# Three feed-forward blocks begun for the first token tile, and a last chunk that skips its round trip

## The chip, the cores and the metric

The kernel runs on one core of one Trainium2 chip. The metric is the device time of one execution in microseconds, taken from several runs, of which the median is quoted. The names of the engines are those of the profile: PE is the matrix engine (TensorE), PEld its weight loads, DVE is VectorE, ACT is ScalarE, POOL is GpSimd, SP is SyncE, which here only issues transfers. Each engine works through its own list of instructions in order and waits on semaphores for the others.

## The reference, cut to what matters

One encoder block with `D_MODEL = 2048`, 256 tokens, all in float32. Two branches (a gated linear attention and a convolution branch called Hyena) are merged, projected, added to the input and normalised; a feed-forward part with a squared ReLU follows.

```python
y_gla = _gla_branch(q, k, v, r, af, ab, ...)
y_hy = _hyena_branch(hy_u, ...)
merged = g[:, :, 0, :] * (y_gla @ w_gla_o[l]) + g[:, :, 1, :] * (y_hy @ w_hy_o[l])
mix = merged @ w_out[l]
h = _layernorm(DEEPNORM_ALPHA * h + mix, ln1_g[l], ln1_b[l])
ff = jnp.square(jax.nn.relu(h @ w_ff1[l])) @ w_ff2[l]
h = _layernorm(DEEPNORM_ALPHA * h + ff, ln2_g[l], ln2_b[l])
```

`w_ff1` is 2048 x 8192 and `w_ff2` 8192 x 2048. The layer norm needs the mean and variance of each token's whole row of 2048 values, so nothing of `h @ w_ff1` can begin for a token before that token's row of `mix` is complete.

## The kernel before, in words

**High and low parts.** Every float32 operand is split in two (`split_hi_lo`, line 82): the high part is a copy in a type that the matrix engine reads fast (an ACT cast, line 83), the low part is the difference to the original (a DVE subtraction, line 84). A product is then three: high by high, high weight by low activation, and low weight by high activation.

**Weights.** They come as 302 blocks of 128 x 2048 (1 MB) through `fetch` (line 91): SP loads a block into one of three `raw` buffers, ACT and DVE split its two halves into three `whi` and three `wlo` buffers of half a block each. `next_block` fetches one block more and hands out the oldest. `resident` (line 838) does the same for blocks that get a place of their own in a slot that is otherwise used for something else.

**Channel products.** With the weights as stationary operand and the activations of both token tiles as moving one, `channel_pair` computes 2 x 128 output channels for all 256 tokens. A block gives 128 channels: 16 high products with 512 moving columns (high and low activation of 256 tokens, line 144) and 16 low products with 256 columns (line 148). `channel_sum` (line 153) adds both column groups. `channel_pair_by_tokens` is a form for the first pair alone: its first one and a half blocks are computed for the first 128 tokens, then again for the second 128, so that high products have 256 columns and low products 128.

**The passage from projection to feed-forward.** The output projection (`wo` in the profile) is done in four groups of 512 output columns. For the last group three blocks are made resident (`x0` and `wr`), so that the first token tile can be finished (`column_products`, lines 885 to 887) before the second. For each token tile follow: `add_mix` (line 901, with the statistics in line 903), `norm_scale` (lines 857 to 861, with the short instructions of lines 214 to 219), five chunks of `norm_chunk` (an ACT scaling in line 868, a DVE product in line 869 and, for the first tile alone, a DVE addition in line 871), and for each chunk `turn`: transposes on PE (line 928; for the second tile also a product that adds the bias, line 932) into a PSUM buffer `ht`, and a split into `hT` (lines 83 and 84). There are four such PSUM buffers (`sdp`) and five chunks. Then `ff1(0)` begins.

**Slots.** The tag `xT` of the pool `base` holds one tile at a time: first the input, then `mT`, the moving operand of the projection, later feed-forward activations. A new tile in the slot waits for the last reader of the one before.

**Order.** The program is written engine-free; a scheduler (`schedule_with_timeline_sim`) sets the order on each engine at build time, except inside `tc.high_priority()`, which moves instructions ahead, and a few fixed places. On the chip the order on each engine is then fixed.

**The Hyena output.** Each of its eight chunks ends in `hy_inv` (line 727): a product on DVE gives `yo`, which goes to DRAM (`yd`) by a POOL transfer. After the gate products `g2` all eight are read back (`yr`) and split into `yhT`, the moving operand of the products `ho`.

## Time and profile before

| | us |
|---|---|
| median of 3 runs | 1862.57 (1861.92 to 1862.78) |
| the profiled execution | 1862.62 |
| its span, first to last instruction | 1860.8 |
| PE busy | 1852.2 |
| DVE busy | 1286.1 |
| ACT busy | 934.5 |

The profiled execution's time is 1.8 us longer than its span: what lies around the first and last instruction. Times in the views are microseconds from the start of the span. The end of a matrix product is modelled by the profile and lies after the start of the next one, so the time that a row of products takes on PE is read from start to start and not from their durations. On DVE and ACT the next instruction starts a little before the end of the one ahead of it, so there too the step is read from start to start.

### The profile page before, as it was taken

Reading aid. Unit: us, or ns where it says so; the run is one execution under the profiler, and the core shown is the slowest. Engines: PE = TensorE matmul, PEld = TensorE weight load, DVE = VectorE, ACT = ScalarE, POOL = GpSimd, SP = SyncE. Lnnn points to the kernel's source line nnn. Section 1 sums busy time; section 2 is a strip of 40 time slices with the busy share of each in tenths; the row PEclk is TensorE's granted clock in tenths of the full one; section 3 lists DMA queues with packets and bytes.
Section 4 is the critical chain, followed back from the end, with each engine's and each line's share of the span. In section 5 each row is a group of like instructions: output and inputs, shape, how many; then the busy total and the mean of one; then the engine's idle time right before and its main releaser. Section 6 shows DMA issues by size and latency. Waiting matters only on the chain.

```text
span 1860.8 us, 23989 instructions
## 1 busy us (share of the span) xinstructions
PE 1852.2 (100%) x9471; PEld 1576.7 (85%) x9471; DVE 1286.1 (69%) x1628; ACT 934.5 (50%) x1268; POOL 30.8 (2%) x61
## 2 busy tenths in 40 slices
PE   9999999999999999999999999999999999999999
PEld 7888888888888888888888889888888888888887
DVE  6787878765788988888645567666555554665557
ACT  5555558765555555555444445444434443444332
POOL 1000000000000000000000000000000000000000
PEclk9999999999999999999999999999999999999999
DMA  7677664445555555566555764555545554545553
GB/s 286 235 251 263 243 233 168 157 159 195 191 199 193 195 217 190 203 218 222 197 188 193 277 219 156 194 209 192 193 186 199 183 197 186 201 184 188 196 192 125
DMA packets 59536, 375.51 MB, mean 202 GB/s; under 512 B 6720, under 2 KB 9184, under 8 KB 20000
## 3 DMA queue, kind: packets, MB, share of 16 engines
q1 hardware_dynamic: 46080, 324.03, 47.2%
q0 software_dynamic: 6288, 30.16, 4.4%
q10 hardware_dynamic: 7056, 19.80, 2.8%
q8 instruction: 74, 1.21, 0.3%
q14 instruction: 38, 0.31, 0.0%
HBM read 357.19 MB, written 16.78 MB: 201 GB/s over the span
## 4 chain that ended last, share of the span: by engine, by line
PE 98%; DVE 1%; DMA 0%; ACT 0%; issue 0%; SPq 0%; DVEq 0%
PE f L144 12%; PE f L148 7%; PE w L198 6%; PE w L197 6%; PE w L196 6%; PE uz L144 3%; PE uv L144 3%; PE ux L144 3%; PE g L196 3%; PE g L198 3%; PE g L197 3%; PE uv L148 2%; PE ux L148 2%; PE uz L148 2%; PE k L144 2%; PE r L196 2%
## 5 line engine op out<-in xcount | busy, mean ns | idle before, releaser
L84 DVE TENSOR_TENSOR wlo<-raw,whi 128x1024 fp32r<-128x1024 f32 x590 | 720.0, 1223 | 351.8 <-ACT whi L83 350.4
L83 ACT CAST whi<-raw 128x1024 fp32r<-128x1024 f32 x590 | 619.6, 1051 | 490.6 <-PE w L198 188.2
L144 PE MATMUL f<-hT,whi 128*128 128x512 f32 (+1 forms) x1048 | 246.4, 386 | 0.0
L144 PEld LDWEIGHTS f<-hT,whi 128*128 128x128 f32 x1048 | 190.1, 188 | 35.6
L197 PE MATMUL w<-wlo,f 128*128 128x512 f32 x480 | 186.7, 389 | 0.0
L198 PE MATMUL w<-whi,f 128*128 128x512 f32 x480 | 186.7, 389 | 0.0
L196 PE MATMUL w<-whi,f 128*128 128x512 f32 x480 | 167.4, 389 | 0.0
L148 PEld LDWEIGHTS f<-hT,wlo 128*128 128x128 f32 x1048 | 134.1, 191 | 4.8
L148 PE MATMUL f<-hT,wlo 128*128 128x256 f32 (+1 forms) x1048 | 135.8, 282 | 0.0
L156 ACT ACTIVATE f_l<-f 128x256 f32<-128x256 f32 x64 | 24.5, 384 | 163.8 <-PE f L144 163.8
L197 PEld LDWEIGHTS w<-wlo,f 128*128 128x128 f32 x480 | 90.1, 188 | 18.7
L196 PEld LDWEIGHTS w<-whi,f 128*128 128x128 f32 x480 | 90.1, 188 | 18.7
L198 PEld LDWEIGHTS w<-whi,f 128*128 128x128 f32 x480 | 90.1, 188 | 18.7
L157 DVE SCALAR_TENSOR_TENSOR f_s<-f,f_l 128x256 f32<-128x256 f32 x64 | 27.2, 425 | 107.1 <-ACT f_l L156 107.1
L197 PE MATMUL g<-wlo,xT 128*128 128x512 f32 x256 | 99.9, 390 | 0.0
L198 PE MATMUL g<-whi,xT 128*128 128x512 f32 x256 | 99.8, 390 | 0.0
L196 PE MATMUL g<-whi,xT 128*128 128x512 f32 x256 | 92.6, 390 | 0.0
L144 PE MATMUL uz<-xT,whi 128*128 128x512 f32 x256 | 63.7, 393 | 0.0
L144 PE MATMUL ux<-xT,whi 128*128 128x512 f32 x256 | 63.6, 391 | 0.0
L144 PE MATMUL uv<-xT,whi 128*128 128x512 f32 x256 | 63.1, 391 | 0.0
L198 PEld LDWEIGHTS g<-whi,xT 128*128 128x128 f32 x256 | 48.1, 188 | 9.9
L197 PEld LDWEIGHTS g<-wlo,xT 128*128 128x128 f32 x256 | 48.1, 188 | 9.8
(399 smaller groups left out, 3189.1 us busy)
## 6 DMA issues: line engine op xcount, KB each, us to landing
raw<-wblk SPq DMA_DIRECT2D x302, 1024.0 KB, 4.8
Td<-T POOLq DMA_DIRECT2D x16, 768.0 KB, 4.0
Tl<-Td POOLq DMA_DIRECT2D x16, 768.0 KB, 4.6
w<-w4s ACTq DMA_DIRECT2D x16, 512.0 KB, 5.2
xw<-first SPq DMA_DIRECT2D x7, 640.0 KB, 10.3
zr<-ln_rows ACTq DMA_DIRECT2D x4, 1024.0 KB, 10.0
dec<-decay_in ACTq DMA_DIRECT2D x8, 256.0 KB, 4.7
yd<-yo POOLq DMA_DIRECT2D x8, 256.0 KB, 3.5
```

The source lines that it names most:

```text
L83: nc.scalar.copy(hi, src)
L84: nc.vector.tensor_tensor(lo, src, hi.bitcast(F32), op=ALU.subtract)
L144: MM(ps[:, :, ts], hi[:, js], act[:, kt, :, ts], start=(kt == 0 and opens), stop=(kt == KT - 1))
L148: MM(ps[:, 0, ts], lo[:, js], act[:, kt, 0, ts], start=False, stop=False)
L156: nc.scalar.activation(low, ps[:, 1], AF.Copy, scale=scale)
L157: nc.vector.scalar_tensor_tensor(dst, ps[:, 0], scale, low, op0=ALU.mult, op1=ALU.add)
L196: MM(pss[tb], sh, wh, start=(kt == 0), stop=False)
L197: MM(pss[tb], sh, wl, start=False, stop=False)
L198: MM(pss[tb], sl, wh, start=False, stop=(kt == KT - 1))
```

## The change

1. `channel_pair_by_tokens` is gone. `ff1(0)` takes three blocks at its beginning: the first from the queue, the next two with `resident` into a tile `wf` in the slot `xT`, which `mT` held. For each of the three, 16 high products for the first token tile are written at once (`high_by_tokens` with tokens 0 to 127).
2. When the pairs come to these three blocks, `channel_pair` adds the high products of the second token tile and then the low products for both tiles together (`low_of_all`).
3. The last Hyena chunk no longer goes through DRAM: `yo` is split directly into `yhT`. The other seven are read back by steps that are queued among the `g2` products, and no longer after them.

```diff
-    def channel_pair(act, name, dst=None, scale=1.0):
+    def channel_pair(act, name, dst=None, scale=1.0, begun=None):
...
         for c in range(2):
-            ps = channel_psum(f"{name}_{c}")
-            parts = next_block()
-            for h in range(2):
-                channel_products(ps, act, parts[h], range(8 * h, 8 * h + 8))
+            if begun:
+                ps, parts = begun.pop(0)
+                high_by_tokens(ps, act, parts, slice(P, L))
+                low_of_all(ps, act, parts)
+            else:
+                ps = channel_psum(f"{name}_{c}")
+                parts = next_block()
+                for h in range(2):
+                    channel_products(ps, act, parts[h], range(8 * h, 8 * h + 8))
...
-    def channel_pair_by_tokens(act, name):
...
+    def high_by_tokens(ps, act, block, ts):
+        for h in range(2):
+            for kt in range(8 * h, 8 * h + 8):
+                MM(ps[:, :, ts], block[h][0][:, kt % 8 * P:(kt % 8 + 1) * P], act[:, kt, :, ts],
+                   start=(kt == 0 and ts.start == 0), stop=False)
+
+    def low_of_all(ps, act, block):
+        for kt in range(KT):
+            MM(ps[:, 0], block[kt // 8][1][:, kt % 8 * P:(kt % 8 + 1) * P], act[:, kt, 0],
+               start=False, stop=(kt == KT - 1))
...
                 nc.vector.tensor_tensor(yo, pt.rearrange("p (a b) -> p a b", a=2), cst.pop(("x2", c)), op=ALU.mult)
+                if c == NCH - 1:
+                    split_hi_lo(yhT[:, 2 * c:, 0], yhT[:, 2 * c:, 1], yo)
+                    return
                 yd = drp.tile([P, 2, L], F32, tag=f"yd{c}", name=f"yd{c}")
...
+    yhT = act_tile(base, "yT", "yh")
+
+    def reload(c):
+        def run():
+            yr = hp.tile([P, 2, L], F32, tag="cv", bufs=2, name=f"yr{c}")
+            nc.gpsimd.dma_start(yr, yh_dram[c])
+            split_hi_lo(yhT[:, 2 * c:2 * c + 2, 0], yhT[:, 2 * c:2 * c + 2, 1], yr)
+        return run
+
+    for c in range(NCH - 1):
+        later(c, reload(c))
     g2_sb = qp.tile([P, 4, NT, 512], F32, tag="G", name="g2_sb")
...
     drain()
-    yhT = act_tile(base, "yT", "yh")
-    for c in range(NCH):
-        yr = hp.tile([P, 2, L], F32, tag="cv", bufs=2, name=f"yr{c}")
-        nc.gpsimd.dma_start(yr, yh_dram[c])
-        split_hi_lo(yhT[:, 2 * c:2 * c + 2, 0], yhT[:, 2 * c:2 * c + 2, 1], yr)
...
     def ff1(qi):
+        begun = []
+        if qi == 0:
+            blocks = [queue.popleft()] + resident(halves(base, "xT", "wf"))
+            fetch()
+            for i, parts in enumerate(blocks):
+                ps = channel_psum(f"f0_{i // 2}_{i % 2}")
+                high_by_tokens(ps, hT, parts, slice(0, P))
+                begun.append((ps, parts))
...
-            r = (channel_pair_by_tokens if qi == 0 and c2 == 0 else channel_pair)(hT, f"f{qi}_{c2}")
+            r = channel_pair(hT, f"f{qi}_{c2}", begun=begun)
```

More of the change, by code (lines that the diff above doesn't have):

```diff
@@ L169, in channel_pair @@
         return dst
-    def channel_pair_by_tokens(act, name):
-        dst = base.tile([P, 2, L], F32, tag="sum", name=f"{name}_s")
-        ps = [channel_psum(f"{name}_{c}") for c in range(2)]
-        blocks = [next_block() for _ in range(2)]
-        for ts in (slice(0, P), slice(P, L)):
-            for c, h in ((0, 0), (0, 1), (1, 0)):
-                channel_products(ps[c], act, blocks[c][h], range(8 * h, 8 * h + 8), ts,
-                                 opens=(c == 0 or ts.start == 0))
-        channel_products(ps[1], act, blocks[1][1], range(8, KT))
-        for c in range(2):
-            channel_sum(dst[:, c], ps[c], f"{name}_l{c}")
-            pump()
-        return dst
+    def high_by_tokens(ps, act, block, ts):
[7 more added lines that the diff above has]
+               start=False, stop=(kt == KT - 1))
     def token_products(pss, act, blocks, tbs, b0):
```

## The prediction

> **What bounds the kernel now.** I read the page first, then who waited for whom on PE, then the passage from projection to feed-forward instruction by instruction on PE, DVE and ACT, then the chain that ended last over the same stretch.

> ```profile
> span 1860.8 us, 23989 instructions
> ...
> PE 1852.2 (100%) x9471; PEld 1576.7 (85%) x9471; DVE 1286.1 (69%) x1628; ACT 934.5 (50%) x1268; POOL 30.8 (2%) x61
> ...
> PE 98%; DVE 1%; DMA 0%; ACT 0%; issue 0%; SPq 0%; DVEq 0%
> ...
> L84 DVE TENSOR_TENSOR wlo<-raw,whi 128x1024 fp32r<-128x1024 f32 x590 | 720.0, 1223 | 351.8 <-ACT whi L83 350.4
> L83 ACT CAST whi<-raw 128x1024 fp32r<-128x1024 f32 x590 | 619.6, 1051 | 490.6 <-PE w L198 188.2
> ```

> PE is the bound almost everywhere: 98% of the chain is PE's, and nothing else fills a per cent except DVE's 1%. So a change pays or costs only in two ways: PE gets more or less to do, or PE has to stand still. The places where PE waits on record are few, and all lie in the opening:

> ```profile
> PE warm L260 <- DVE ones_sb L293: 1.5, 1, 1.5
> PE mlp L329 <- issue: 1.5, 1, 1.5
> ```

> (Columns: us in total, times, longest.) The passage shows no wait in that view only because modelled ends of products overlap short gaps. The chain names it: between these two groups of PE rows it runs through DVE and ACT.

> ```profile
> 1137.93 0.34 DVE hT L84
> ...
> 1138.59 0.60 DVE zr L871
> ...
> 1140.12 0.34 DVE bst L903
> 1140.46 0.59 DVE hT L84
> 1141.05 0.28 DVE mv L857
> ...
> 1142.68 0.17 DVE lnb L861
> ...
> 1148.10 1.44 PE f L144 x12
> 1149.54 1.29 PE f L148 x12
> ...
> 1160.17 3.65 PE f L144 x16
> 1163.83 1.91 PE f L148 x16
> 1165.74 3.65 PE f L144 x16
> ```

> (Columns: start, time on the chain, what.) This gives all steps that I need. DVE is packed here: a 256-column step takes 0.34, a 512-column step 0.60, the statistics' end 0.28. On PE a product with 512 columns takes 3.65/16 = 0.228, one with 256 columns 1.44/12 = 0.120 (high) or 1.91/16 = 0.120 (low), but one with 128 columns 1.29/12 = 0.1075: halving the columns of a low product saves a tenth, not a half.

> ```profile
> 1137.38 0.28 PE L887 MATMUL wo<-wr,mT 128*128 128x256 f32 x1
> 1137.50 1.25 PE L928 MATMUL ht<-ident,zr 128*128 128x128 f32 x10
> 1138.51 0.72 PE L144 MATMUL f<-hT,whi 128*128 128x256 f32 x4
> ...
> 1144.82 0.41 PE L928 MATMUL ht<-ident,zr 128*128 128x128 f32 x2
> ...
> 1147.94 1.60 PE L144 MATMUL f<-hT,whi 128*128 128x256 f32 x12
> 1149.37 1.46 PE L148 MATMUL f<-hT,wlo 128*128 128x128 f32 x12
> ```

> The last projection product starts at 1137.38. From 1138.51 PE works on the first token tile, then turns the second tile, and from 1147.94 (1148.10 on the chain) works without a hole.

> **The Hyena part: zero.** The change removes two transfers of 256 KB (write and read back) from POOL's queue; the seven other reloads keep their order there.

> ```profile
> L196 PE MATMUL ho<-whi,yh x128: 389/389/393, 958.4 to 1047.4; 128*128 128x512 f32 x128
> ...
> L84 DVE TENSOR_TENSOR yh<-yr,yh x8: 682/685/693, 870.2 to 920.8; 128x512 fp32r<-128x512 f32 x8
> ```

> The last split starts at 920.8 and its first user at 958.4: 37 us of cover, PE's products that do not read `yh`. The scheduler had spread the reloads from 870.2 on before the source did. Without the cover eight DVE differences of 0.69 would be exposed, 5.5 us, but no split moves later by 37 us. I take nothing.

> **PE's work on three blocks: 2.0 us less.** Before, blocks one and two take 48 high products of 256 columns, 48 low ones of 128, and 8 + 8 undivided ones; block three 16 + 16 undivided. After, 96 high of 256 and 48 low of 256. Before: 48 x 0.120 + 48 x 0.1075 + 24 x 0.228 + 24 x 0.120 = 19.3; after: 144 x 0.120 = 17.3.

> **What DVE must do first: the cost.** The two extra blocks go into the slot of `mT`, whose last reader is the product at 1137.38. So ACT cannot cast them before 1137.5, just when both norms are on DVE and ACT. In the order in which the built program stands, all four casts of `wf` come ahead of the first tile's `hT` casts on ACT, and all four differences ahead of the first `hT` difference on DVE.

> ```profile
> 1118.77 2.35 DVE L84 TENSOR_TENSOR wr<-raw,wr 128x1024 fp32r<-128x1024 f32 x2
> ...
> 1117.32 2.00 ACT L83 CAST wr<-raw 128x1024 fp32r<-128x1024 f32 x2 [1.83 <-DMA raw<-wblk]
> ...
> 1128.00:1130.00 2.00, 2.00 (x19) 2.00 (x18) 1.08 (x3) 0.00 (x0) 0.00 (x0) 1.00 0.03 12
> ...
> 1130.73 0.22 DVE L217 SCALAR_TENSOR_TENSOR lq_t<-lq_y,lq_v 128x1 f32<-128x1 f32 x1 [0.41 <-ACT lq_y L215]
> ...
> 1133.17 0.42 DVE L901 SCALAR_TENSOR_TENSOR zr<-zr,wo 128x256 f32<-128x256 f32 x1 [0.53 <-PE wo L887]
> ```

> (The third row is of the view by stretches: busy time of PE, PEld, DVE, ACT and POOL, granted clock, share of the transfers.) Two such differences take 2.35 with one tail, a single one 1.22 in the page's group, so 1.13 to 1.14 a step; two casts 2.00, a single one 1.05, so 0.95. No transfer is waited for: the three `raw` buffers were filled before, and from 1128 the transfers stand still (share 0.03). Now the walk.

> 1. Up to the end of the first tile's last addition (line 871, until 1139.2 on the chain) DVE's list holds nearly the same pieces; the fourth block's first difference moves in among the short norm instructions (1.14, of which 0.4 falls into an idle stretch), and DVE's list meets PE again at line 901, which waits until 1133.17 for a projection product in both orders. I take 1139.1, as now.
> 2. Then come four differences (4.56), one statistics step (0.34) and the statistics' end (0.28): 5.2. The ACT casts (1137.5 to 1141.3) stay just ahead. So the first `hT` difference starts at 1144.3 or 1144.4, not at 1137.93: 6.4 later.
> 3. PE's order after the last projection product is: four chunks' transposes, the fifth chunk's, then the high products. The fifth chunk needs the first chunk's PSUM buffer, whose last reader is that `hT` difference. PE stands from about 1138.9 (last transposes that can run) to 1144.4 + 0.42 + a little = 1144.9: **6.0 us idle**, where it now works on `f` from 1138.51.
> 4. DVE goes on: four `hT` differences (0.34 + 0.34 + 0.60 + 0.60), two short ones (0.35), the fifth difference (0.60), two short ones (0.35): `lnb` of the second tile at 1147.5 instead of 1142.68. From there to the second tile's products it now takes 1148.10 - 1142.68 = 5.4, which would make 1152.9.
> 5. PE alone needs longer: from 1144.9 it has four transposes (0.4), 48 high products (5.8) and the second tile's turn. That turn (16 transposes at 1.25/10 less the tail, about 0.11; two products of 256 columns and three of 512) is 2.6. Together 8.8, so the second tile's products begin at 1153.7: 5.6 later than now.
> 6. After that point the old order has, to the end of block four, 8 x 0.228 of the row at 1165.74, that is 1167.57 - 1148.10 = 19.5. The new has 48 x 0.120 + 48 x 0.120 + 16 x 0.348 = 17.1. That gives back 2.4.

> Sum at full clock: +5.6 - 2.4 = **+3.2 us**. Behind it PE is packed to the end, and nothing gives this back. The later release of `whi` buffers (low products now come last) is covered: block four's second half is split about 7 us before its products by the same steps; without that cover its 2.3 would show.

> **The clock after a standstill.** The trace shows what a pause costs beyond itself.

> ```profile
> 26.19 0.67 PE L329 MATMUL mlp<-emb_sb,mlpw 33*128 33x256 f32 x2 [1.48 <-issue]
> 26.79 2.65 PE L144 MATMUL q<-xT,whi 128*128 128x512 f32 x8
> 29.24 3.11 PE L148 MATMUL q<-xT,wlo 128*128 128x256 f32 x16
> 32.18 2.00 PE L144 MATMUL q<-xT,whi 128*128 128x512 f32 x8
> ...
> 28.17:31.58 3.41, 3.41 (x15) 0.50 0.30 71
> ```

> (Last row: the view by stretches, PE busy, number, granted clock.) After an idle gap of 1.48 the granted clock was 0.50 for 3.41 us, although PE had resumed. 8 products of 512 and 16 of 256 took 32.18 - 26.79 = 5.39, where 8 x 0.228 + 16 x 0.120 = 3.74 is usual: 1.65 lost. A gap of 6.0 is four times that one. PE's 8.8 us from 1144.9 are packed, so half clock there goes straight into the end. Bounds: 0 (clock back before PE resumes) and 2.5 (one and a half such stretches after resuming). I take 1.5, near the one row there is, slightly under it because part of the stretch may fall into the standstill.

> [...]

> Forecast: 1862.62 (the profiled execution, 0.05 above the median of the runs) + 3.2 + 1.5 = **1867.3 us**, slower by 0.25%. A measurement of this kernel can tell about 0.2% from no change, 3.7 us, so up to 1866.3 counts as the same.

> **Rivals.**
> - *The stall is not there or short (faster).* If the `wf` differences come so early, or PE's wait is so loose, that the first `hT` difference starts less than about 2.4 us later than now, the gain in work outweighs; with no stall at all it is 1862.6 - 2.0 = 1860.6. For it: DVE is not full before 1133 (1.08 of the 2 us from 1128). Against: the slot of `mT` is read until 1137.5, and each engine's order is fixed. It decides at a first `hT` difference before 1140.3.
> - *The stall is there but the clock stays full.* 1862.6 + 3.2 = 1865.8, not to be told from no change. For it: there is one half-clock row only, in the opening. Against: that row's gap was shorter.
> - *Half clock twice, or a longer stall.* A second pause on PE while the second tile is turned (its chunks come one by one from ACT and DVE, which are late too) would add another half stretch: 1867.3 + 1.7 to 2.5, 1869 to 1870. Against: PE's own list is as long as that passage (8.8 against 8.0).

> **How the numbers follow.** Forecast (stall and half clock, 1866.3 to 1869.2) 0.70; full clock 0.15; no stall 0.07; more than 1869.2 0.08. The range 1865.3 to 1869.2 takes in the first two: its low end is +3.2 with half a microsecond off for seams in the walk, its high end is +3.2 + 2.5 with 0.9 for seams. Slower by over 0.2%: 0.70 + 0.08 = 0.78; within: 0.15; faster: 0.07.

> **What would show it.** In the changed profile: the four `wf` differences on DVE between 1139 and 1144.5 and the first `hT` difference behind them; a gap on PE of about 6 us before the fifth chunk's transposes; a stretch of 3.4 us with granted clock 0.50 near 1141 to 1148; `f` products of the second tile from about 1154 or 1155; block four ending at about 1172; `ho` starting at 958 as now. Wrong I would be if the first `hT` difference stays near 1138, if PE's gap is filled with `f` products, or if no row has clock 0.50.

## The result, and the profile after

| | before | after |
|---|---|---|
| median, 12 runs each | 1861.81 us | 1866.76 us |
| lowest to highest | 1859.41 to 1864.84 | 1864.7 to 1871.75 |
| profiled execution | 1862.62 | 1866.93 |
| its span | 1860.8 | 1865.1 |

The ratio is 1.003, with an interval from 1.0022 to 1.0038: the changed kernel is slower by 4 to 7 us (the medians lie 4.95 apart), where +4.7 was forecast.

On the page of the changed kernel PE's busy time is what it was (1852.2 before), although the span is 4.3 us longer: the time went into standing still.

```profile
PE 1851.4 (99%) x9471; PEld 1576.5 (85%) x9471; DVE 1285.9 (69%) x1628; ACT 934.6 (50%) x1268; POOL 29.8 (2%) x59
```

Who waited for whom on PE (us in total, times, longest) names the place. Its longest row is new; the two others lie in the opening, as before.

```profile
PE ht L939 <- DVE hT L84: 5.7, 1, 5.7
```

DVE and PE of the changed kernel in the passage from projection to feed-forward (start, duration, engine, line, operation), first DVE:

```profile
1138.20 0.69 DVE L882 TENSOR_TENSOR zr<-zr 128x512 f32<-128x512 f32 x1
1138.80 1.22 DVE L84 TENSOR_TENSOR wf<-raw,wf 128x1024 fp32r<-128x1024 f32 x1
1139.94 0.42 DVE L914 BATCH_NORM_STATS2 bst<-zr 128x6 f32<-128x256 f32 x1
1140.28 2.34 DVE L84 TENSOR_TENSOR wf<-raw,wf 128x1024 fp32r<-128x1024 f32 x2
1142.54 0.37 DVE L868 BATCH_NORM_AGGREGATE mv<-bst 128x2 f32<-128x48 f32 x1
1142.82 1.16 DVE L84 TENSOR_TENSOR wf<-raw,wf 128x1024 fp32r<-128x1024 f32 x1
1143.89 1.94 DVE L84 TENSOR_TENSOR hT<-ht,hT 128x256 fp32r<-128x256 f32 x4
...
1147.12 0.16 DVE L872 SCALAR_TENSOR_TENSOR lnb<-mv,lrs 128x1 f32<-128x1 f32 x1
```

then PE:

```profile
1136.73 0.28 PE L898 MATMUL wo<-wr,mT 128*128 128x256 f32 x1
1136.85 1.82 PE L939 MATMUL ht<-ident,zr 128*128 128x128 f32 x12
1144.36 1.11 PE L939 MATMUL ht<-ident,zr 128*128 128x128 f32 x4 [5.70 <-DVE hT L84]
...
1154.60 0.64 PE L179 MATMUL f<-hT,whi 128*128 128x256 f32 x4
```

Four `wf` differences stand ahead of the first `hT` difference (1143.89), and the fifth chunk's transposes wait 5.70 for that one. The chain that ended last (start, time on the chain, what) runs through exactly these:

```profile
1142.90 1.08 DVE wf L84
1143.98 0.34 DVE hT L84
...
1144.36 1.11 PE ht L939 x4
1145.47 4.93 PE f L179 x34
...
1154.76 1.44 PE f L179 x12
...
1170.02 3.65 PE f L144 x16
```

The clock (view by stretches of the changed kernel: length, busy time of PE, PEld, DVE, ACT and POOL, granted clock, share and rate of the transfers):

```profile
1137.07:1140.48 3.41, 1.47 (x12) 0.99 (x10) 3.41 (x7) 3.41 (x4) 0.00 (x0) 1.00 0.00 0
1140.48:1143.89 3.41, 0.00 (x0) 0.00 (x0) 3.41 (x4) 2.47 (x7) 0.00 (x0) 0.50 0.33 89
1143.89:1147.31 3.42, 2.95 (x14) 2.95 (x15) 3.20 (x11) 0.59 (x1) 0.00 (x0) 0.50 1.00 410
1147.31:1150.72 3.41, 3.41 (x32) 3.41 (x31) 2.40 (x5) 3.22 (x5) 0.00 (x0) 1.00 0.28 115
```

Half clock from 1140.48 to 1147.31, two stretches of 3.41. They lie on one grid with the half-clock stretch that this kernel has in the opening, at 10.67: (1140.48 - 10.67)/331 = 3.4133. PE was busy for 2.95 of the two stretches. In the row of the opening that the prediction shows, half clock lost 1.65 of 3.41, about half; by that I put the loss here at 2.95/2 = 1.5 us.

**A measure for the experiments.** The time up to the passage differs from profile to profile, also between kernels that have the same code there: the last `wo` product starts at 1133.80 in one of them and at 1138.61 in another (table below). So spans of single profiles don't compare to some tenths of a per cent, and I take the passage alone: from the start of the last `wo` product to the start of the first `w` product (line 198; 196 before). What was changed in the feed-forward lies between them; the Hyena part lies ahead of them. Each passage is that of one profiled execution. At full clock it repeats well: the kernel before and the one with the Hyena part alone have the same code in the passage and differ by 0.01. Its end before (first row) and after:

```profile
1323.29 0.39 PE L196 MATMUL w<-whi,f 128*128 128x512 f32 x1
```

```profile
1327.57 0.39 PE L198 MATMUL w<-whi,f 128*128 128x512 f32 x1
```

| kernel | last `wo` | first `w` | passage against before | PE busy at half clock | ratio of times |
|---|---|---|---|---|---|
| before | 1137.38 | 1323.29 | 0 | 0 | 1 |
| after | 1136.73 | 1327.57 | +4.93 | 2.95 | 1.003 |
| Hyena part alone | 1138.04 | 1323.94 | -0.01 | 0 | 1.0001 |
| blocks alone | 1134.67 | 1326.45 | +5.87 | 5.10 | 1.0032 |
| differences late | 1136.01 | 1325.38 | +3.46 | 5.56 | 1.0013 |
| gap filled | 1137.40 | 1326.96 | +3.65 | 0 | 1.0024 |
| casts between | 1138.61 | 1324.63 | +0.11 | 0 | 0.9997 |
| one extra block | 1137.33 | 1324.70 | +1.46 | 0 | 1.0004 |
| no extra block | 1133.80 | 1321.54 | +1.83 | 3.31 | 1.0008 |
| early casts | 1136.86 | 1320.39 | -2.38 | 0 | 0.9986 |
| scheduler's order | 1134.60 | 1327.10 | +6.59 | 6.15 | 1.0028 |

Of the time in the fifth column I count half as lost where PE is what the passage waits for, and less where the norm is. (At half clock four products of 256 columns took 0.85, from 1143.62 to 1144.47 with the differences late, where 4 x 0.120 = 0.48 is usual.)

### The profile page after: what moved, and what is told of

It is laid out like the page before. It is cut to its first block, busy times and chain, and to the rows that moved or that the text cites. A ratio compares the mean times of both kernels' runs of the same rounds, so it can differ in the third digit from the quotient of the medians.

```text
span 1865.1 us, 23979 instructions
## 1 busy us (share of the span) xinstructions
PE 1851.4 (99%) x9471; PEld 1576.5 (85%) x9471; DVE 1285.9 (69%) x1628; ACT 934.6 (50%) x1268; POOL 29.8 (2%) x59
## 3 DMA queue, kind: packets, MB, share of 16 engines
q8 instruction: 74, 1.21, 0.3%
## 4 chain that ended last, share of the span: by engine, by line
PE 90%; issue 7%; DVE 1%; DMA 1%; POOL 0%; SPq 0%; DVEq 0%; POOLq 0%
PE f L144 12%; PE f L148 6%; PE w L200 6%; PE w L199 6%; PE w L198 6%; PE uz L144 3%; PE uv L144 3%; PE ux L144 3%; PE g L200 3%; PE g L199 3%; PE g L198 3%; PE uv L148 2%; PE ux L148 2%; PE uz L148 2%; PE go L198 2%
## 5 line engine op out<-in xcount | busy, mean ns | idle before, releaser
L84 DVE TENSOR_TENSOR wlo<-raw,whi 128x1024 fp32r<-128x1024 f32 x586 | 715.1, 1223 | 353.8 <-ACT whi L83 348.3
L83 ACT CAST whi<-raw 128x1024 fp32r<-128x1024 f32 x586 | 615.4, 1051 | 489.3 <-PE w L200 188.0
L144 PE MATMUL f<-hT,whi 128*128 128x512 f32 x976 | 233.5, 391 | 0.0
L144 PEld LDWEIGHTS f<-hT,whi 128*128 128x128 f32 x976 | 179.3, 188 | 34.6
L198 PE MATMUL w<-whi,f 128*128 128x512 f32 x480 | 167.4, 389 | 0.0
L148 PEld LDWEIGHTS f<-hT,wlo 128*128 128x128 f32 x976 | 125.1, 191 | 4.8
L148 PE MATMUL f<-hT,wlo 128*128 128x256 f32 x976 | 126.6, 283 | 0.0
L198 PEld LDWEIGHTS w<-whi,f 128*128 128x128 f32 x480 | 90.1, 188 | 18.8
L198 PE MATMUL g<-whi,xT 128*128 128x512 f32 x256 | 92.6, 390 | 0.0
L144 PE MATMUL uz<-xT,whi 128*128 128x512 f32 x256 | 63.7, 393 | 0.0
L144 PE MATMUL ux<-xT,whi 128*128 128x512 f32 x256 | 63.6, 391 | 0.0
L144 PE MATMUL uv<-xT,whi 128*128 128x512 f32 x256 | 63.1, 391 | 0.0
```

What stands on the lines that cost most here:

```text
L83: nc.scalar.copy(hi, src)
L84: nc.vector.tensor_tensor(lo, src, hi.bitcast(F32), op=ALU.subtract)
L144: MM(ps[:, :, ts], hi[:, js], act[:, kt, :, ts], start=(kt == 0 and opens), stop=(kt == KT - 1))
L148: MM(ps[:, 0, ts], lo[:, js], act[:, kt, 0, ts], start=False, stop=False)
L198: MM(pss[tb], sh, wh, start=(kt == 0), stop=False)
```

## The experiments

The theory: the Hyena part is worth nothing, the new order of the products saves about 2.4 us behind the second norm, and the four `wf` differences in front of the norm cost more than that: a standstill of PE, a later norm, and half clock behind the standstill. The rivals: the cost lies in the Hyena part, in the products themselves, or in the clock alone.

### The two parts apart

The Hyena edit alone put into the kernel before, and the changed kernel with the Hyena edit taken out:

```diff
+                if c == NCH - 1:
+                    split_hi_lo(yhT[:, 2 * c:, 0], yhT[:, 2 * c:, 1], yo)
+                    return
...
+    for c in range(NCH - 1):
+        later(c, reload(c))
```

> The kernel before with the Hyena edit alone (seven reloads queued among the g2 products, the last chunk split directly). Stall theory (the time comes from the wf differences on DVE): no difference, within 1 us, because the last yh split lies 37 us ahead of its first user; the last split moves some 10 us earlier and PE does not see it. Rival (the Hyena edit costs part of the 5 us, by reloads that crowd DVE and ACT during g2): 1 to 5 us slower, and PE rows with waits between 860 and 960.

> The changed kernel with the Hyena part as before. Stall theory: the whole +5 us (4 to 6, by where the clock's grid falls), PE gap of 5.7 us before the fifth chunk's transposes. Rival (part comes from the Hyena edit): clearly less than +5.

Measured: Hyena alone 1.0001 (0.9992 to 1.001), blocks alone 1.0032 (1.0019 to 1.0045). So the Hyena part costs and saves nothing that these runs can tell from zero. The passage says nothing of it, because the Hyena part lies ahead of the passage. From the first `g` product to the last `wo` product, a stretch that takes the Hyena part in, the kernel before needs 1137.38 - 356.2 = 781.2 us and Hyena alone 1138.04 - 356.9 = 781.1. In the changed kernel the last chunk's split (first row; second row the first user of `yh`) lies 47 us ahead of its use, where the last split before lay 37 us ahead:

```profile
L84 DVE TENSOR_TENSOR yh<-yo,yh x1: 687/687/687, 910.9 to 910.9; 128x512 fp32r<-128x512 f32 x1
...
L198 PE MATMUL ho<-whi,yh x128: 389/389/393, 957.9 to 1047.0; 128*128 128x512 f32 x128
```

The passage of blocks alone took 0.9 more than that of the changed kernel. Its gap was the same (5.70); PE spent 5.10 us at half clock in place of 2.95, which is 1.1. The half-clock share is thus a matter of the single execution as well as of the kernel. The twelve runs of the changed kernel fit that: their mean granted clock goes from 0.998 down to 0.996, and the lowest belongs to the longest run, 1871.75.

### The differences moved behind the norm

```diff
-            blocks = [queue.popleft()] + resident(halves(base, "xT", "wf"))
+            with tc.issue_after(turned[1][1].ins):
+                wf = resident(halves(base, "xT", "wf"))
+            blocks = [queue.popleft()] + wf
```

(`turned[1][1]` is the second tile's last `hT` difference. ACT keeps its order.)

> The changed kernel, with the four wf differences on DVE queued behind the second tile's last hT difference; the four casts on ACT stay where they are, ahead of the hT casts, and the slot of mT stays. Stall theory: DVE no longer holds up hT, only ACT does, by four casts of 0.95; the gap on PE shrinks from 5.7 to about 3, the second norm comes earlier by about 4 us, and the time is 1 us under the kernel before at full clock, up to 0.5 over it with half clock after the gap. Rival (the cost is PE's own: products of three blocks interleaved, or block four's buffers released late): still +4 to +5, since PE's list holds the same products. Rival (the cost is the wait for the slot of mT): still +4 to +5.

Measured: 1.0013 (1.0004 to 1.0021), passage +3.46. I had forecast from 1 us faster to 0.5 us slower, and missed. PE's wait became shorter, as forecast, and did not vanish; the row of waits of this kernel:

```profile
PE ht L940 <- DVE hT L84: 3.0, 1, 3.0
```

DVE now waits for ACT, whose four `wf` casts still stand ahead of the `hT` casts:

```profile
1140.52 2.05 DVE L84 TENSOR_TENSOR hT<-ht,hT 128x256 fp32r<-128x256 f32 x4 [1.41 <-ACT hT L83]
...
1144.00 0.16 DVE L872 SCALAR_TENSOR_TENSOR lnb<-mv,lrs 128x1 f32<-128x1 f32 x1
```

`lnb` comes 8.0 after the last `wo` (1144.00 - 1136.01), where it came 10.4 after it in the changed kernel and 5.3 before: 2.4 earlier, and not the 4 that I had counted on. Half clock followed all the same, and 5.56 us of PE's work fell into it, so up to 2.8 of the 3.46 are the clock's. Without that the passage would be 0.7 longer than before, against 3.4 (4.93 - 1.5) for the changed kernel: by this working, which takes half clock as lost in full, the four differences carry 2.7 of the 3.4, and ACT's casts the rest.

### The gap filled with products that nobody reads

The changed kernel with 22 products of 512 columns, whose result nobody reads, between the fourth and the fifth chunk's transposes: PE has something to do while it waits.

```diff
             norm_chunk(z1, rows1, tb, at, n, rs, nb)
+            if tb == 0 and at == 1536:
+                pf = psum_main("fill")
+                for _ in range(22):
+                    tc.keep_in_program_order(MM(pf, x0[0][:, 0:P], x0[0][:, 0:512], start=True, stop=True))
             turn(at, n)
```

> The changed kernel with 22 products of 512 columns whose result nobody reads (5.0 us) on PE between the fourth and the fifth chunk's transposes, into a PSUM buffer that is free there. It fills the standstill and moves nothing else. Theory that the standstill also halves the clock afterwards: no row with clock 0.50 near 1140 to 1148, the 34 high products that follow at 0.12 each, and 1.5 us less than the changed kernel, +3.3 to +3.5 over the kernel before. Rival (half clock costs nothing, because the second norm is the bound then): same time as the changed kernel, +5.

Measured: 1.0024 (1.0015 to 1.0033), passage +3.65. PE worked for all but 0.66 us of the time until it could go on, the granted clock stayed at 1.00, and the second tile's products came at 1153.98, 16.6 after the last `wo` (17.9 in the changed kernel, 10.6 before).

```profile
1139.09 5.29 PE L952 MATMUL fill<-xh 128*128 128x512 f32 x22
1145.03 0.66 PE L939 MATMUL ht<-ident,zr 128*128 128x128 f32 x4 [0.66 <-DVE hT L84]
...
1153.98 0.40 PE L179 MATMUL f<-hT,whi 128*128 128x256 f32 x2
```

So half clock is worth 4.93 - 3.65 = 1.3 us in this passage, and 3.65 is lost without it. The rival that it is all the clock falls. The 1.3 rests on one passage of each kernel: the ratios of the two, 1.0024 and 1.003, have intervals that overlap.

### Casts between the norm's steps

Differences behind the second tile's last `hT` difference, as above, and the casts, too, out of the first tile's way: those of the second block behind the first tile's last `hT` cast, those of the third behind the second norm's square root.

```diff
+            with tc.issue_after(turned[0][0].ins), tc.issue_after(turned[1][1].ins):
+                blocks += resident([slots[0]])
+            with tc.issue_after(roots[1].ins), tc.issue_after(turned[1][1].ins):
+                blocks += resident([slots[1]])
```

> The changed kernel with the four wf differences behind the second tile's last hT difference, the casts of the second block behind the first tile's last hT cast, and those of the third behind the second tile's square root on ACT. Stall theory: no gap on PE over 0.5 us, clock full, second norm about 1 us later than in the kernel before, 2.4 us less work behind it and a little idle time gone: 3 us faster than the kernel before (2 to 3.5). Rival (three-block form costs on PE by itself): slower than the kernel before or equal.

Measured: 0.9997 (0.9988 to 1.0006), passage +0.11. The gain that I expected did not come. There was no gap over 0.5 us and no half clock, but ACT's rows show what I had missed: two casts stand ahead of the second norm's square root, and two between the root and the scaling of the second tile.

```profile
1142.39 2.00 ACT L83 CAST wf<-raw 128x1024 fp32r<-128x1024 f32 x2
...
1144.72 1.98 ACT L83 CAST wf<-raw 128x1024 fp32r<-128x1024 f32 x2
1146.60 3.21 ACT L881 ACTIVATE zr<-zr,lnb,lrs 128x256 f32<-128x256 f32 x5
```

The scaling starts 1146.60 - 1138.61 = 8.0 after the last `wo`, where it was 5.5 before (1142.88 - 1137.38), and the second tile's products come at 1151.66, 13.05 after it and not 10.56. These 2.5 eat the 2.4 that the new order saves. Four casts of 0.95 have no place inside the norm on ACT.

### Fewer blocks

The changed kernel with one extra block in place of two, and with none (only the block from the queue is begun early):

```diff
-            blocks = [queue.popleft()] + resident(halves(base, "xT", "wf"))
+            slots = halves(base, "xT", "wf")
+            blocks = [queue.popleft()]
+            blocks += resident([slots[0]])
```

(the last line is left out in the second of the two)

> The changed kernel with only one extra block in the slot of mT (two blocks begun), order left to the scheduler. Stall theory: two differences and two casts instead of four, 2.3 us less on DVE ahead of hT; the gap on PE about 3 us, the time between 1.7 us faster (full clock) and equal to the kernel before (half clock after the gap). Rival (each resident block costs the same): half of +5.

> The changed kernel with no extra block (one block begun from the queue), so that only the undivided low products of that block remain of the change. Stall theory: no wf differences, norms as in the kernel before, no gap over 2 us, and 0.0 to 2.3 us faster, by the low products that have 256 columns now. Rival (the undivided low products leave PE idle during the second norm by as much as they save): equal to the kernel before.

Measured: one extra block 1.0004 (0.9995 to 1.0012), none 1.0008 (0.9999 to 1.0017), passages +1.46 and +1.83. I had expected no loss or a gain, and missed by 1.5 to 4 us. DVE's `lnb` of the second tile and PE's first product of that tile with one extra block:

```profile
1144.76 0.16 DVE L874 SCALAR_TENSOR_TENSOR lnb<-mv,lrs 128x1 f32<-128x1 f32 x1
```

```profile
1150.01 0.40 PE L179 MATMUL f<-hT,whi 128*128 128x256 f32 x2
```

and with none, with the stretches in which PE waits for the second norm:

```profile
1139.10 0.16 DVE L874 SCALAR_TENSOR_TENSOR lnb<-mv,lrs 128x1 f32<-128x1 f32 x1
```

```profile
1145.11 0.40 PE L179 MATMUL f<-hT,whi 128*128 128x256 f32 x2
```

```profile
1137.43:1140.85 3.42, 1.83 (x11) 1.43 (x11) 2.46 (x10) 2.06 (x5) 0.00 (x0) 1.00 0.00 0
1140.85:1144.26 3.41, 3.31 (x15) 2.75 (x14) 2.87 (x6) 2.76 (x6) 0.00 (x0) 0.50 0.00 0
```

With one, the norm is 2.1 late (`lnb` 7.43 after the last `wo`, before 5.30) and the products 2.1 (12.68, before 10.56). Behind them stand two begun blocks, 2 x 32 x 0.120, and two whole ones, 2 x 16 x 0.348: 18.8 where before had 19.5. That makes +2.1 - 0.7 = +1.4, and 1.46 was measured. With none the norm is not late at all (5.30 again). But PE has half its time free before it, half clock follows while it turns the second tile, and the products come 0.75 later (11.31). Behind them stand one begun block and three whole ones, 20.5, 1.0 more than before: 0.75 + 1.0 = 1.8. Before, the divided low products filled the wait; what is taken out of a wait and put behind it costs its whole duration, however well it is packed there. The rival that each resident block costs the same falls too: with none, one and two of them the passages are +1.83, +1.46 and +4.93.

### Early casts, and the same without a fixed order

The second norm leaves no room on ACT and little on DVE; before the norms, ACT has room. So the high halves of all three blocks are cast early into the six ordinary half-block buffers (three `whi`, three `wlo`), and only the low halves, which are needed late, go into the slot of `mT`: six DVE differences behind the second tile's last `hT` difference.

```diff
-            fetch()
+            early = high_halves(3)
...
-            blocks = [queue.popleft()] + resident(halves(base, "xT", "wf"))
+            with tc.issue_after(turned[1][1].ins):
+                blocks = low_halves(early)
```

(`high_halves` loads three blocks and casts their halves, `low_halves` makes the six differences; the first replaces the fetch in the second tile's turn of the projection.) The second kernel is the same without the line `with tc.issue_after(...)`: each engine has the same work, and the scheduler chooses the order. On PE that order hardly differs: by the names of their tiles 24 of the 9471 products stand in another place, all of them among those of the three blocks.

> The changed kernel with the casts and the differences of the first three blocks put apart in time: the high halves of all three are cast before the two norms into the ordinary weight buffers, and the low halves (six differences of 1.14 on VectorE) are made later, behind the second tile's last hT difference, in the slot of mT. Theory (the loss is the four wf differences ahead of the first hT difference, with TensorE's standstill and half clock behind it; the saved products and the later low ones are a gain once nothing delays the norm): no gap on TensorE over 1.5 us in the passage, full clock, the second tile's products as early after the last projection product as before (10.6 us), and 17.1 instead of 19.5 us of products behind them: 2.3 less than before in the passage, about 1859.5 where before takes 1861.8, and 7 less than the changed kernel. Rival A (the products in their new order cost more than they save, whatever the norm does): no faster than before, 1862 to 1864. Rival B (the six late differences come too late for the low products): a new wait on TensorE behind the high products of the second tile, 2 to 4 us, 1861.5 to 1863.5.

> The same kernel as the run before it, with the one line left out that puts the six low differences behind the second tile's last hT difference: the scheduler is then free and puts them ahead of the first hT difference on VectorE. The work of every engine is the same. Theory (stall): a gap of about 5.6 us on TensorE ahead of the fifth chunk's transposes, the norm later by six differences less what falls into idle time, 5.0 more than before in the passage at full clock and 5.5 to 7 with half clock behind the gap: 1867 to 1869, 7.3 to 9.3 more than with the line. Rival A (cost lies in the products, not in the order on VectorE): within 1 us of the run with the line.

Measured: early casts 1859.82 us beside 1862.08 for the kernel before, ratio 0.9986 (0.9977 to 0.9994), passage -2.38; without the line 1866.8, ratio 1.0028 (1.0017 to 1.0038), passage +6.59. The passages are as the theory had them (2.3 less; 5.5 to 7 more), the time of the second kernel is a little under what I gave, and one line lies between the two kernels. DVE of the kernel with the line:

```profile
1137.33 0.42 DVE L84 TENSOR_TENSOR hT<-ht,hT 128x256 fp32r<-128x256 f32 x1
...
1142.16 0.16 DVE L899 SCALAR_TENSOR_TENSOR lnb<-mv,lrs 128x1 f32<-128x1 f32 x1
...
1148.85 3.48 DVE L885 TENSOR_TENSOR wf<-raw,whi 128x1024 fp32r<-128x1024 f32 x3
1152.25 3.49 DVE L885 TENSOR_TENSOR wf<-raw,wlo 128x1024 fp32r<-128x1024 f32 x3
```

and its PE:

```profile
1136.86 0.28 PE L925 MATMUL wo<-wr,mT 128*128 128x256 f32 x1
...
1147.42 0.64 PE L179 MATMUL f<-hT,whi 128*128 128x256 f32 x4
...
1162.69 3.82 PE L144 MATMUL f<-hT,whi 128*128 128x512 f32 x16
```

`lnb` comes 5.30 after the last `wo` and the second tile's products 10.56 after it, both as before, and block four ends at 1162.69 + 8 x 0.228 = 1164.5, 17.1 later, where the order before needs 19.5. PE has no row of waits in the passage, so the six late differences do not come too late (rival B). The kernel without the line, first the waits of PE:

```profile
PE f L179 <- DVE hT L84: 5.3, 1, 5.3
```

This wait is not where I had put it. One `hT` difference still ran ahead of the six, so the fifth chunk's transposes got their PSUM buffer, and PE stood behind them, before the `f` products that need the next `hT` differences. Then DVE, on which the sixth difference ends where the next `hT` difference begins:

```profile
1139.74 3.48 DVE L885 TENSOR_TENSOR wf<-raw,wlo 128x1024 fp32r<-128x1024 f32 x3
1143.14 1.01 DVE L84 TENSOR_TENSOR hT<-ht,hT 128x256 fp32r<-128x256 f32 x2
...
1147.19 0.16 DVE L899 SCALAR_TENSOR_TENSOR lnb<-mv,lrs 128x1 f32<-128x1 f32 x1
```

and the clock, by the view of stretches:

```profile
1139.52:1149.76 10.24, 6.15 (x29) 6.15 (x30) 8.68 (x18) 2.88 (x6) 0.00 (x0) 0.50 0.79 307
```

Here `lnb` comes 12.59 after the last `wo`, 7.3 late, which less the 2.4 makes 4.9 at full clock, as forecast (5.0); half clock adds the other 1.7 of the 6.59, less than half of 6.15. I take it that part of the half clock lies where PE waits for the norm in any case; no run shows that apart.

That the new products cost more than they save falls with the first kernel, and that the order on DVE does not matter with the second. The kernel with early casts beats both given kernels: the one before by 0.14%, the changed one by 0.4%, if the two ratios are divided (0.9986 / 1.003 = 0.9956).

## Why the prediction was right, point by point

- **The Hyena part, zero.** Shown within the interval of the runs, 0.9992 to 1.001, and in the profiles by the stretch that takes it in, 781.2 and 781.1.
- **PE's work, 2.0 less, and 2.4 given back behind the second tile.** The 2.4 is shown; the 2.0, of which it is the part behind the second tile, was not read by itself. On the chain the products from the second tile to the end of block four take from 1154.76 to 1170.02 + 8 x 0.228 = 1171.84, 17.1 as worked out; early casts confirm it without the stall.
- **The walk on DVE.** The first tile's last addition ended at 1138.9 (forecast 1139.1), the first `hT` difference began at 1143.89 (1144.3 or 1144.4), `lnb` at 1147.12 (1147.5). The last `wo` was 0.65 earlier in this execution, so counted from it each came 0.2 to 0.45 later than forecast.
- **PE's standstill, 6.0.** It was 5.70. That it comes from differences ahead of those of `hT` on DVE is shown twice: with the differences moved away the wait fell to 3.0, and in the last pair one line of order on DVE made 9.0 of the passage (6.59 + 2.38). That PE waits for the fifth chunk's PSUM buffer is what the profile of the changed kernel names; in the kernel with the scheduler's order the same delay held PE one step later.
- **The sum at full clock, +3.2.** The kernel with the filled gap has full clock and +3.65; the changed kernel less its half-clock loss has 3.4. So the walk was 0.2 to 0.45 short. PE's own list of 8.8 took 8.95 with the gap filled, from 1145.03 to 1153.98.
- **Half clock, +1.5.** 1.3 by the filled gap, 1.5 by the busy time at half clock. The size was right and its working was not: I had one stretch of 3.41 in mind; there were two, of which the first fell wholly into the standstill. That the size came so close to 1.5 is in part luck: half of the 5.10 in blocks alone is 2.6, just over the upper bound of 2.5, after the same wait of 5.70.
- **The rivals.** No stall: excluded by 5.70. Full clock throughout: excluded by the rows with 0.50, though it is where the filled gap lies (1.0024). A second pause in the second tile's turn: no row of waits has one.

One thing the prediction did not see: it booked ACT's casts as staying "just ahead" of the differences and so as free. They are the second obstacle in their own right. The kernel with late differences keeps a wait of 3.0, behind ACT, and casts between the norm's steps cost 2.5.

## What to carry to other kernels

Work that is handed to a resident buffer has to be split by other engines first, and the slot that it goes into says when: here the slot came free just as the norm, a stretch in which PE depends on DVE and ACT, began. Before filling PE's idle time with more work, ask when its operands can be made and what stands behind that on their engines; casting early and subtracting late turned +4.9 us of the passage into -2.4. Where a scheduler sets the order, one explicit line of order can be worth more than the change.

## What the runs showed of the hardware that I had not expected

```profile
1136.32:1139.73 3.41, 1.51 (x12) 1.03 (x10) 2.72 (x7) 3.40 (x4) 0.00 (x0) 1.00 0.00 0
1139.73:1143.15 3.42, 2.15 (x10) 2.16 (x11) 2.42 (x5) 2.88 (x8) 0.00 (x0) 0.50 0.00 0
```

In the opening of the kernel before it was 1.98, just ahead of the one row that the prediction had:

```profile
24.76:28.17 3.41, 1.98 (x8) 1.45 (x9) 1.62 (x3) 2.27 (x3) 0.00 (x0) 1.00 0.92 375
```

But with one extra block there was a stretch with less than that, 1.68, and full clock behind it (1.00 from 1144.26 to 1147.67). (The grid there is continued from that kernel's own half-clock stretch at 11.03, in steps of 3.4133.)

```profile
1140.85:1144.26 3.41, 1.68 (x14) 1.68 (x15) 3.30 (x7) 0.98 (x3) 0.00 (x0) 1.00 0.32 86
```

Between 1.7 and 2.0 us the busy time thus does not decide alone, and what else does stays open; the ends of products are modelled, and transposes are counted as busy here.

In these profiles the way back to full clock took a fuller stretch than the fall. At half clock, a stretch with 2.95 us busy was followed by full clock (the changed kernel, 1143.89 to 1147.31), but one with 2.15 by another at half clock (differences late, second row above), and so was one with 2.74 in the kernel with the scheduler's order:

```profile
1142.93:1146.35 3.42, 2.74 (x13) 2.74 (x14) 3.17 (x8) 0.33 (x2) 0.00 (x0) 0.50 1.03 410
```

Half clock lasted 3.41 us (the opening of the kernel before), 6.83 (the changed kernel) and 10.24 (the scheduler's order): one, two and three steps of the grid. The stretches right ahead of it had 1.21 to 1.98 us of work in five profiles. Where the grid lies against a gap differs from profile to profile: the last transposes ahead of the wait ended at 1136.85 + 1.82 = 1138.67 in the changed kernel and at 1134.79 + 1.82 = 1136.61 in blocks alone, and half clock began at 1140.48 and 1140.58, 1.8 and 4.0 later. So the same wait of 5.70 put 2.95 us of PE's work at half clock once and 5.10 another time.
